# Two modulation vectors from plain float32 products, four channel chunks in the column groups of the array

## The chip, the core and the metric

The kernel is one program on one core of a Trainium2 chip. The metric is the device time of one execution in microseconds (us), here as the median of three runs. In the text PE is TensorE, DVE is VectorE, ACT is ScalarE, POOL is GpSimd and SP the engine that issues most loads. Numbers of the form L570 are lines of the kernel before; where the changed kernel is meant, the text says so.

## The reference, cut to what matters

The model is two transformer-like blocks on 256 tokens of width 2048 (and 256 context tokens). The change concerns its first step, the modulation: two conditioning vectors, `c` and `c_ctx`, go through SiLU and are multiplied with `w_mod`. Of the six vectors of 2048 that come out, the first two (shift and scale of the first norm) are needed for both conditioning vectors, before anything else can be projected:

```python
sil = silu([c, c_ctx])                        # 2 x 2048
mod = sil @ w_mod[:, 0:4096] + b_mod[0:4096]  # shift, scale: 2 x 2048 each
h   = rmsnorm(x,   norm1_w) * (1 + scale[0]) + shift[0]    # 256 x 2048
hc  = rmsnorm(ctx, norm1_w) * (1 + scale[1]) + shift[1]
p   = h @ w_in + b_in                         # q, k, v, gates of the mixer; same for hc
```

The result has to agree with float32 products. The kernel gets them in two ways: by splitting each operand into a high part in the type float32r and a rest, and adding three products of the parts; or by handing float32 operands to the array as they are.

## The kernel before, in words

Phase A, the first 198 us, is all that the change edits. `w_mod`'s first 4096 columns are stored as eight blocks of 512 columns, `wmodA[0..7]`; block b and block 4 + b are shift and scale of the same 512 channels. `mod_block(b)` goes through the 2048 input channels in 16 steps k of 128. Its weights come by `wstream`, a generator that loads four k at a time (`raw`, 128 x 4 x 512, one MB, L162, on the SP queue) and splits each k: ACT casts it to `whi` (L117) and DVE subtracts to get `wlo` (L118); both have four buffers. The stationary operand is `silx`, 128 x 4: high and low part of the two conditioning vectors. PE multiplies it with `whi` (L570) and with `wlo` (L571), 512 columns each, so that four rows of a PSUM bank hold the sums. ACT copies these to `mrow` (L573), and `mod_cols` turns them into columns by four small transposes (L579) and adds the parts and the bias on DVE (L581, L583).

The loop over the four channel chunks c calls `mod_block(c)`, `mod_block(4 + c)` and then queues `early(c)`, which does two things. `h_chunk(c)` makes the modulated `hTh` (ACT, L603), the same in float32 in place (POOL, L604) and the rest `hTl` (DVE, L605), eight instructions of each. Then four k of the first half of the key projection and four of the query projection follow (`ws_ka`, `ws_qa`): 24 and 12 products of 256 columns for each k, L189, 144 products a chunk. Before the first chunk `x_norm` loads x and ctx, scales them, and turns them by transposes (L207).

What stands where on each engine is set by a scheduler that takes the program's pieces in the order in which they are queued, and by buffers: 16 pages of 8 KB a partition (`page`), 2 `raw` buffers (`stm`), 19 small ones (`t2`), and 4 + 4 PSUM banks (`mmb`, `smb`). An engine does its instructions in the order of its own queue. `half_step` and `rate` say how many queued pieces are emitted with each k.

Of the kernel before, what the change touches and what calls it, by code (L numbers as in the profile page):

```python
# [33 lines left out]
def body(ctx, tc, A, out):  # L34
# [69 lines left out]
    def sq_part(ss, x, tt, j):  # L104
        """sum of squares of column block j of x[tt]"""
        junk = t2([128, 512], F32, "junk")
        nc.scalar.activation(out=junk[:], in_=x[tt][:, j * 512:j * 512 + 512], func=AF.Square, accum_out=ss[:, tt, j:j + 1])
# [12 lines left out]
    def due(then, X, at):  # L120
        """X, with then() emitted when its k first reaches at"""
        todo = [then]

        def X_(k, i):
            if todo and k >= at:
                todo.pop()()
            return X(k, i)

        return X_

    def warm(func):
        """the table of func, ahead of its use"""
        t = wk.tile([128, 1], F32, name="warm", tag="warm")
        tc.keep_in_program_order(nc.scalar.activation(out=t[:], in_=ones[:], func=func))
# [4 lines left out]
    def pump(n=1):  # L139
        """emit the next n pieces of the work that runs beside the weight streams"""  # L140
        for lane in lanes:
            m = n
            while m > 0 and lane:
                try:
                    with tc.issue_after(last_split[0].ins) if paced[0] else ExitStack():
                        next(lane[0])
                    m -= 1
                except StopIteration:
                    lane.pop(0)
# [59 lines left out]
    def token_row(r, name):  # L209
        """r [128, 2], tokens on partitions, as a row of 256 on every partition"""  # L210
        ps = smb()
        for tt in range(2):
            nc.tensor.matmul(ps[:, tt * 128:tt * 128 + 128], lhsT=r[:, tt:tt + 1].to_broadcast([128, 128]), rhs=ident[:],
                             start=True, stop=True)
        t = t2([128, 256], F32, name)
        nc.vector.tensor_copy(out=t[:], in_=ps[:, 0:256])
        return t

    def turned(xs, j):
        """column block j of xs, channel-major: two banks of two chunks"""  # L220
        for k2 in range(j * 4, j * 4 + 4, 2):
            ps = smb()
            for k in range(2):
                for tt in range(2):
                    transpose(ps[:, k * 256 + tt * 128:k * 256 + tt * 128 + 128],
                              xs[tt][:, (k2 + k) * 128:(k2 + k) * 128 + 128])
            yield k2, ps
# [14 lines left out]
    def chan_part(xs, j, gcol, chan):  # L242
        """column block j of xs with a factor per channel, channel-major and split"""
        for k2, ps in turned(xs, j):
            for k in range(2):
                kk = k2 + k
                (h_, l_), p_ = chan(kk, 0), ps[:, k * 256:k * 256 + 256]
                nc.scalar.activation(out=h_, in_=p_, func=AF.Copy, scale=gcol[:, kk:kk + 1])
                nc.vector.scalar_tensor_tensor(out=l_, in0=p_, scalar=gcol[:, kk:kk + 1], in1=h_.bitcast(F32),
                                               op0=OP.mult, op1=OP.subtract)  # L250

# [47 lines left out]
    def s5_prep():  # L299
# [23 lines left out]
        def horner(o, x, coefs, last):  # L323
            """o = (...((c0 x + c1) x + c2)...) x + last"""
            ts(o, x, coefs[0], None, OP.mult)
            for c_ in coefs[1:]:
                V.scalar_tensor_tensor(out=o, in0=o, scalar=c_, in1=x, op0=OP.add, op1=OP.mult)
            ts(o, o, last, None, OP.add)
# [51 lines left out]
        # unit rotation and decay of four steps, and the rotations at the starts of the chunks  # L380
# [34 lines left out]
        # powers of the transition  # L415
# [9 lines left out]
        # input coefficients  # L425
# [20 lines left out]
    def s5_prep2():  # L446
# [12 lines left out]
        # parity of the step: rows of a block-diagonal factor for two groups, and the products by lag after zeros  # L459
# [46 lines left out]
        for e in range(16):  # L506
# [15 lines left out]
            # with the conjugate of c its table is the one of Re(c z) up to the sign of the imaginary part  # L522
# [32 lines left out]
    silx = cst.tile([128, 16, 4], F32R, name="silx")  # L555
    split(silx[:, :, 0:2], silx[:, :, 2:4], sil[:])
# [9 lines left out]
    def mod_block(b):  # L566
        """512 modulation columns for both vectors, channel-major; high and low parts as rows of one product"""
        ps = smb()
        for k, wh, wl in wstream(A["wmodA"][b], 16, rawp=page if b else raw_first):
            nc.tensor.matmul(ps[0:4, :], lhsT=silx[:, k, :], rhs=wh, start=(k == 0), stop=False)  # L570
            nc.tensor.matmul(ps[0:4, :], lhsT=silx[:, k, :], rhs=wl, start=False, stop=(k == 15))  # L571
        mrow = t2([4, 512], F32, "mrow")
        nc.scalar.copy(out=mrow[:], in_=ps[0:4, :])  # L573
        bg.append(mod_cols(b, mrow))

    def mod_cols(b, mrow):
        pt = smb()
        for j in range(4):
            nc.tensor.transpose(pt[:, j * 4:j * 4 + 4], mrow[:, j * 128:(j + 1) * 128], ident[0:4, 0:4])  # L579
        p4 = pt[:, 0:16].rearrange("p (a b) -> p a b", b=4)  # L580
        nc.vector.tensor_tensor(out=modc[:, b], in0=p4[:, :, 0:2],  # L581
                                in1=bmod[:, b * 4:b * 4 + 4, None].to_broadcast([128, 4, 2]), op=OP.add)
        nc.vector.tensor_tensor(out=modc[:, b], in0=modc[:, b], in1=p4[:, :, 2:4], op=OP.add)  # L583
# [4 lines left out]
    def h_chunk(c):  # L588
        """channels 512 c .. 512 c + 511 of the modulated x and ctx"""
# [27 lines left out]
    # the first projections follow the modulation, chunk by chunk  # L617
# [41 lines left out]
    def mod_vector(v):  # L659
        """c-modulation vector v (2..5), as a row in memory; the scale of the second norm with its weight"""  # L660
# [34 lines left out]
    def mod_narrow(v, accs, step, eng):  # L695
        """the same in column blocks, up to the sums over partitions"""
# [93 lines left out]
    # differential attention  # L790
# [69 lines left out]
    def normed_turn(o, ss, factor, hi, lo, slow):  # L860
        """o scaled by its head norm and factor(tt, h), channel-major and split"""
# [14 lines left out]
    def to_chan(src, nk, hi, lo):  # L876
        """src(k, tt) token-major [128, 128] chunks -> hi/lo channel-major pages [128, nk, 256]"""
# [68 lines left out]
    # gate rows: direction * 32 + head on partitions, all 512 tokens  # L946
# [214 lines left out]
    def mod_col(v, name):  # L1161
        """modulation vector v by channel: [128, 16]"""
# [99 lines left out]
    # dense activations gelu(h2 . u), [i2, i1, t], two first keys i1 per unit, by way of memory  # L1262
# [20 lines left out]
    # slot[:, 0/1/2, t]: first key, second key and weight of each of a token's 128 slots, slots on partitions  # L1283
# [57 lines left out]
    def scatter(half, G):  # L1341
        """G[i2, i1, t] for 64 first keys: per token the product of the slots' one-hot rows, the weights in exact parts"""
# [33 lines left out]
    class Half:  # L1376
        """the products with expert_v of 64 first keys"""
# [38 lines left out]
        def run(self, done, after):  # L1416
            """the last two rows column block by column block, so that the ends of the blocks are spread"""
# [35 lines left out]
    def first_half():  # L1453
        """the first half's part of x2, once its gate is there"""
# [37 lines left out]
    # the norm that ends the first block and the one that begins the second, from two sums of squares  # L1492
# [35 lines left out]
    # 1 / rms of the first norm, and of both in one  # L1528
# [58 lines left out]
    # forget gates of the forgetting attention  # L1587
# [9 lines left out]
    # decay of the gated linear attention, channel-major  # L1597
# [33 lines left out]
    # gated linear attention: pairs (s, t) split by the level of the halving at which s and t part  # L1631
# [56 lines left out]
    # forgetting attention  # L1688
# [30 lines left out]
    # head norm of the gated linear attention, gates  # L1719
# [35 lines left out]
    def s5_v(h):  # L1755
        """the table of the inputs' part of the states of 16 groups, and what else s5_in needs"""
# [85 lines left out]
    def s5_u(h):  # L1842
        """u by (group of the pair, token in chunk from the last, channel of the group)"""
# [10 lines left out]
    def s5_in(h):  # L1854
        """states at the ends of the chunks of 4 tokens, of 16 groups"""
# [40 lines left out]
    def s5_out(h, U, X):  # L1896
        """outputs within and across chunks"""
# [25 lines left out]
    def s5_y(h):  # L1923
        """back to channels, skip and gelu"""
# [98 lines left out]
def _layout(inp):  # L2023
# [82 lines left out]
    # channels of 8 groups of 16 in the order (channel of the group, group)  # L2106
# [7 lines left out]
    # groups as (16 channel blocks in pairs, 8): a pair is the same group of the two blocks  # L2114
# [11 lines left out]
    # shape-only constants  # L2126
# [49 lines left out]
```

## Time and profile before

| what | value |
|---|---|
| median of three runs | 3814.56 us (3808.14 to 3821.2) |
| profiled execution | span 3811.4 us from its first to its last instruction; no other time is given for it |
| PE | busy 95% of the span, 24610 products |
| DVE | busy 72% |
| ACT | busy 49% |
| POOL | busy 21% |
| DMA | 754.22 MB, mean 198 GB/s |
| phase A, to the last product of the first query projection | 198.14 us |

A share over the whole span says little on phase A: there PE is busy 157.8 of 198.14 us, and the waits are in a few places. A product's row gives a duration that includes the filling and draining of the array; how often products follow each other is read from their starts. A plain float32 product leaves two records in the trace, one for each of two passes.

### The profile page before, as it was taken

The page shows a single profiled execution, that of the slowest core. Times are in us where ns is not written, and L with a number is a line of the kernel's source. Part 1 is how long each engine was busy: PE and PEld are TensorE (multiplying, and loading weights), DVE is VectorE, ACT ScalarE, POOL GpSimd, SP SyncE. Part 2 cuts the span into 40 slices and gives each one's busy share as a digit, 9 for nine tenths or more (in the row PEclk, how much of TensorE's full clock was granted, in tenths as well). Part 3 has the DMA queues.
Part 4 walks back from the last instruction along what each step waited for, and adds up shares of the span by engine and source line. Part 5 has one row for each costly group of instructions (what it writes and reads, how often), then busy time and mean ns, then how long its engine had stood idle before and what let it go on. Part 6 is the DMA issues. An engine that isn't in the chain of part 4 may idle for free.

```text
span 3811.4 us, 65434 instructions
## 1 busy us (share of the span) xinstructions
PE 3638.0 (95%) x24610; PEld 3172.0 (83%) x24610; DVE 2744.6 (72%) x4697; ACT 1859.4 (49%) x3748; POOL 792.1 (21%) x778
## 2 busy tenths in 40 slices
PE   7899999999999999999999998899999999988998
PEld 4698878887789999999877888888879977787896
DVE  6765897777658687887787589866577676676765
ACT  7622544654455444555545445554454445433464
POOL 1211210100101022554011057300032021242300
PEclk8999999999999999999999999999999999999999
DMA  8464564367654555555667534666545635776554
GB/s 329 175 241 171 179 234 151 110 247 292 236 198 146 196 197 188 199 189 190 240 232 257 189 136 161 241 219 212 193 162 190 204 116 177 214 202 188 156 194 166
DMA packets 155246, 754.22 MB, mean 198 GB/s; under 512 B 40609, under 2 KB 40897, under 8 KB 76465
## 3 DMA queue, kind: packets, MB, share of 16 engines
q1 hardware_dynamic: 116224, 661.78, 49.4%
q0 software_dynamic: 29232, 84.07, 6.9%
q10 hardware_dynamic: 9472, 4.20, 0.4%
q8 instruction: 192, 3.15, 0.3%
q14 instruction: 126, 1.02, 0.1%
HBM read 716.65 MB, written 33.19 MB: 197 GB/s over the span
## 4 chain that ended last, share of the span: by engine, by line
PE 77%; DVE 9%; DMA 5%; issue 3%; POOL 3%; ACT 3%; DVEq 0%; ACTq 0%; POOLq 0%; SPq 0%
PE mm L189 15%; PE mm L180 7%; PE mm L183 7%; PE mm L181 7%; PE sm L1273 5%; PE sm L1274 5%; PE sm L1278 5%; PE mm L1414 3%; PE sm L1411 3%; PE mm L1411 3%; PE sm L1414 3%; PE sm L1412 3%; PE mm L1412 3%; DVE wlo L118 3%; POOL oh L1354 1%
## 5 line engine op out<-in xcount | busy, mean ns | idle before, releaser
L118 DVE TENSOR_TENSOR wlo<-raw,whi 128x512 fp32r<-128x512 f32 x2224 | 1647.7, 760 | 833.8 <-ACT whi L117 745.6
L117 ACT CAST whi<-raw 128x512 fp32r<-128x512 f32 x2224 | 1349.2, 620 | 1613.6 <-PE mm L181 333.3
L1273 PE MATMUL sm<-h2h,whi 128*128 128x256 f32 x2048 | 514.2, 283 | 0.5 <-ACT whi L117 0.5
L1274 PE MATMUL sm<-h2l,whi 128*128 128x256 f32 x2048 | 509.0, 282 | 0.0
L1273 PEld LDWEIGHTS sm<-h2h,whi 128*128 128x128 f32 x2048 | 388.0, 189 | 0.7 <-ACT whi L117 0.7
L1274 PEld LDWEIGHTS sm<-h2l,whi 128*128 128x128 f32 x2048 | 387.7, 189 | 0.0
L1278 PE MATMUL sm<-h2h,wlo 128*128 128x256 f32 x2048 | 327.5, 282 | 10.3 <-DVE wlo L118 10.3
L1354 POOL TENSOR_TENSOR oh<-e,gpart 128x512 bf16<-128x512 bf16 x192 | 281.7, 1491 | 136.9 <-ACT whi L117 62.4
L1278 PEld LDWEIGHTS sm<-h2h,wlo 128*128 128x128 f32 x2048 | 279.8, 189 | 11.7 <-DVE wlo L118 11.5
L180 PE MATMUL mm<-whi,hTh 128*128 128x512 f32 x576 | 229.6, 399 | 0.7 <-ACT whi L117 0.4
L181 PE MATMUL mm<-whi,hTl 128*128 128x512 f32 x576 | 227.0, 394 | 0.0
L189 PE MATMUL mm<-hTh,whi 128*128 128x256 f32 x704 | 178.9, 289 | 6.0 <-ACT whi L117 3.5
L189 PE MATMUL mm<-hTl,whi 128*128 128x256 f32 x704 | 175.7, 284 | 0.0
L183 PE MATMUL mm<-wlo,hTh 128*128 128x512 f32 x576 | 172.6, 397 | 1.5 <-DVE wlo L118 1.4
L189 PEld LDWEIGHTS mm<-hTh,whi 128*128 128x128 f32 x704 | 134.4, 191 | 15.7 <-ACT whi L117 5.3
L189 PE MATMUL mm<-cnh,whi 128*128 128x256 f32 x512 | 137.4, 300 | 3.6 <-ACT whi L117 3.6
L189 PEld LDWEIGHTS mm<-hTl,whi 128*128 128x128 f32 x704 | 134.7, 192 | 3.2 <-issue 1.5
L180 PEld LDWEIGHTS mm<-whi,hTh 128*128 128x128 f32 x576 | 108.5, 188 | 30.2 <-issue 3.4
L183 PEld LDWEIGHTS mm<-wlo,hTh 128*128 128x128 f32 x576 | 108.1, 189 | 28.3 <-DVE wlo L118 3.6
L189 PE MATMUL mm<-cnl,whi 128*128 128x256 f32 x512 | 131.0, 288 | 0.0
L181 PEld LDWEIGHTS mm<-whi,hTl 128*128 128x128 f32 x576 | 108.5, 188 | 23.3
L1281 POOL DMA_DIRECT2D scr_a<-ua x64 | 36.3, 567 | 432.7 <-ACT ua L1280 421.3
(1564 smaller groups left out, 7949.8 us busy)
## 6 DMA issues: line engine op xcount, KB each, us to landing
raw<-in_u_t_dram SPq DMA_DIRECT2D x128, 1024.0 KB, 4.8
raw<-in_expert_v_dram SPq DMA_DIRECT2D x124, 1024.0 KB, 4.8
raw<-in_w_in_dram SPq DMA_DIRECT2D x80, 1024.0 KB, 4.9
raw<-in_ab_w_in_dram SPq DMA_DIRECT2D x56, 1024.0 KB, 4.9
raw<-in_wmodA_dram SPq DMA_DIRECT2D x32, 1024.0 KB, 7.2
mraw<-in_wmodB_dram SPq DMA_DIRECT2D x32, 1024.0 KB, 8.4
raw<-in_c_w_in_dram SPq DMA_DIRECT2D x32, 1024.0 KB, 5.1
mrn<-in_wmodB_dram POOLq DMA_DIRECT2D x64, 256.0 KB, 3.9
```

Source lines behind the costliest of these rows:

```text
L117: nc.scalar.copy(out=hi, in_=src)
L118: last_split[0] = nc.vector.tensor_tensor(out=lo, in0=src, in1=hi.bitcast(F32), op=OP.subtract)
L180: nc.tensor.matmul(o, lhsT=xh, rhs=wh, start=(k == 0), stop=False)
L181: nc.tensor.matmul(o, lhsT=xl, rhs=wh, start=False, stop=False)
L183: nc.tensor.matmul(ps[i][:], lhsT=X(k, tt)[0], rhs=wl, start=False, stop=(k == K - 1))
L189: nc.tensor.matmul(o, lhsT=w[:, j * 128:(j + 1) * 128], rhs=x, start=start, stop=stop, skip_group_check=True)
L1273: nc.tensor.matmul(o, lhsT=uh, rhs=xh, start=(k == 0 and r == 0), stop=False, skip_group_check=True)
L1274: nc.tensor.matmul(o, lhsT=uh, rhs=xl, start=False, stop=False, skip_group_check=True)
L1278: nc.tensor.matmul(o, lhsT=w_, rhs=x_, start=False, stop=(k_ == 15 and r == 1), skip_group_check=True)
L1354: nc.gpsimd.tensor_tensor(out=oh1[i][:], in0=e1[:], in1=gpart[:, i, tb:tb + 8, None].to_broadcast([128, 8, 64]), op=OP.mult)
L1411: nc.tensor.matmul(self.ps[tt][b][:], lhsT=hl[tt][0], rhs=vh, start=first, stop=False)
L1412: nc.tensor.matmul(self.ps[tt][b][:], lhsT=hl[tt][1], rhs=vh, start=False, stop=False)
```

## The change

`silx` with its split goes. A zeroed operand `silz` of 32 columns for each k, of which two hold the conditioning vectors, takes its place. `mod_block` loads the same `raw` pieces in the same order on the same queue, but multiplies them unsplit, in float32: the four k of a piece go to four groups of 32 columns of the array, and their sums to four groups of 32 partitions of one bank. `mod_cols` then transposes four full 128 x 128 blocks, and adds up the four groups in a DVE reduction. The rest of the diff takes comments and docstrings away. After phase A, the order of the instructions on each engine is the same in both kernels.

```diff
-    silx = cst.tile([128, 16, 4], F32R, name="silx")
-    split(silx[:, :, 0:2], silx[:, :, 2:4], sil[:])
+    silz = t2([128, 16, 32], F32, "silz")
+    nc.gpsimd.memset(silz[:], 0.0)
+    nc.vector.tensor_copy(out=silz[:, :, 0:2], in_=sil[:])
...
     def mod_block(b):
         ps = smb()
-        for k, wh, wl in wstream(A["wmodA"][b], 16, rawp=page if b else raw_first):
-            nc.tensor.matmul(ps[0:4, :], lhsT=silx[:, k, :], rhs=wh, start=(k == 0), stop=False)
-            nc.tensor.matmul(ps[0:4, :], lhsT=silx[:, k, :], rhs=wl, start=False, stop=(k == 15))
-        mrow = t2([4, 512], F32, "mrow")
-        nc.scalar.copy(out=mrow[:], in_=ps[0:4, :])
+        for k4 in range(0, 16, 4):
+            raw = (page if b else raw_first)("raw", [128, 4, 512])
+            nc.sync.dma_start(out=raw[:], in_=A["wmodA"][b][:, k4:k4 + 4, :])
+            for k in range(4):
+                half_step[0] += rate[0] / 2
+                pump(int(half_step[0]))
+                half_step[0] -= int(half_step[0])
+            for k in range(4):
+                nc.tensor.matmul(ps[32 * k:32 * k + 32, :], lhsT=silz[:, k4 + k, :], rhs=raw[:, k, :], start=(k4 == 0),
+                                 stop=(k4 == 12), tile_position=(0, 32 * k), skip_group_check=True)
+        mrow = t2([128, 512], F32, "mrow")
+        nc.scalar.copy(out=mrow[:], in_=ps[:])
         bg.append(mod_cols(b, mrow))
 
     def mod_cols(b, mrow):
         pt = smb()
         for j in range(4):
-            nc.tensor.transpose(pt[:, j * 4:j * 4 + 4], mrow[:, j * 128:(j + 1) * 128], ident[0:4, 0:4])
-        p4 = pt[:, 0:16].rearrange("p (a b) -> p a b", b=4)
-        nc.vector.tensor_tensor(out=modc[:, b], in0=p4[:, :, 0:2],
-                                in1=bmod[:, b * 4:b * 4 + 4, None].to_broadcast([128, 4, 2]), op=OP.add)
-        nc.vector.tensor_tensor(out=modc[:, b], in0=modc[:, b], in1=p4[:, :, 2:4], op=OP.add)
+            transpose(pt[:, j * 128:(j + 1) * 128], mrow[:, j * 128:(j + 1) * 128])
+        nc.vector.tensor_reduce(out=modc[:, b], in_=pt[:].rearrange("p (j g v) -> p j v g", j=4, g=4)[:, :, 0:2, :],
+                                axis=AX.X, op=OP.add)
+        nc.vector.tensor_tensor(out=modc[:, b], in0=modc[:, b], in1=bmod[:, b * 4:b * 4 + 4, None].to_broadcast([128, 4, 2]),
+                                op=OP.add)
         yield
```

PE in the first chunk's key projection, before: between projection products (`hTh`, `hTl` with `whi`, `wlo`; the numbers name buffers) stand pairs of modulation products, one pair for each k.

```order
L189 MATMUL mm<-hTh_544,wlo 128x256
L189 MATMUL mm<-hTh_542,wlo 128x256
L189 MATMUL mm<-hTh_544,wlo 128x256
L570 MATMUL sm<-whi,silx 4x512
L571 MATMUL sm<-wlo,silx 4x512
L570 MATMUL sm<-whi,silx 4x512
L571 MATMUL sm<-wlo,silx 4x512
L189 MATMUL mm<-hTh_542,whi 128x256
```

PE in the same projection, changed kernel (its L578 are the modulation products, straight from `raw`).

```order
L189 MATMUL mm<-hTh_376,wlo 128x256
L189 MATMUL mm<-hTh_378,wlo 128x256
L189 MATMUL mm<-hTh_376,wlo 128x256
L189 MATMUL mm<-hTh_378,wlo 128x256
L578 MATMUL sm<-raw,silz 32x512 x4
L189 MATMUL sm<-hTh_376,whi 128x256
```

The pairs are gone; a whole piece of four k stands as one run of four products.

DVE at the start of the first chunk, before: after the scale `amod` the rests `hTl` of the modulated input, and between them splits `wlo` of weights.

```order
L591 SCALAR_TENSOR_TENSOR amod<-modc,nw_79 128x8
L118 TENSOR_TENSOR wlo<-raw,whi 128x512 x2
L605 TENSOR_TENSOR hTl_543<-xnT_87,hTh_542 128x256
L605 TENSOR_TENSOR hTl_545<-xnT_89,hTh_544 128x256
L605 TENSOR_TENSOR hTl_543<-xnT_87,hTh_542 128x256
L605 TENSOR_TENSOR hTl_545<-xnT_89,hTh_544 128x256
L118 TENSOR_TENSOR wlo<-raw,whi 128x512 x4
L605 TENSOR_TENSOR hTl_543<-xnT_87,hTh_542 128x256
L605 TENSOR_TENSOR hTl_545<-xnT_89,hTh_544 128x256
L118 TENSOR_TENSOR wlo<-raw,whi 128x512 x2
L605 TENSOR_TENSOR hTl_543<-xnT_87,hTh_542 128x256
```

DVE at the same place in the changed kernel, from `amod` of the first chunk to the first reduction of the second (its L599, L613 and L588).

```order
L599 SCALAR_TENSOR_TENSOR amod<-modc,nw_79 128x8
L613 TENSOR_TENSOR hTl_377<-xnT_87,hTh_376 128x256 x2
L613 TENSOR_TENSOR hTl_379<-xnT_89,hTh_378 128x256 x2
L613 TENSOR_TENSOR hTl_377<-xnT_87,hTh_376 128x256
L613 TENSOR_TENSOR hTl_379<-xnT_89,hTh_378 128x256
L613 TENSOR_TENSOR hTl_377<-xnT_87,hTh_376 128x256
L613 TENSOR_TENSOR hTl_379<-xnT_89,hTh_378 128x256
L118 TENSOR_TENSOR wlo<-raw,whi 128x512 x8
L588 TENSOR_REDUCE modc<-sm 128x8
```

Only the eight splits of the projections' own weights are left, and they stand behind all `hTl` of the chunk.

## Rows read from the trace of the kernel before

**Rows 1.** The page: the span, and each engine's busy time over it.
```profile
span 3811.4 us, 65434 instructions
PE 3638.0 (95%) x24610; PEld 3172.0 (83%) x24610; DVE 2744.6 (72%) x4697; ACT 1859.4 (49%) x3748; POOL 792.1 (21%) x778
```

**Rows 2.** Busy time by stretch, cut at each chunk's first `hTh`; last: clock, DMA, GB/s.
```profile
0.00:56.66 56.66, 34.64 (x138) 15.55 (x138) 30.75 (x73) 41.34 (x92) 8.97 (x20) 0.82 0.97 385
56.66:100.68 44.02, 37.35 (x221) 25.70 (x222) 32.35 (x57) 30.20 (x56) 8.05 (x10) 0.88 0.72 261
100.68:137.66 36.98, 33.64 (x216) 23.37 (x215) 29.17 (x53) 26.81 (x49) 10.45 (x10) 1.00 0.65 238
137.66:178.49 40.83, 33.18 (x212) 23.38 (x210) 29.68 (x53) 28.01 (x50) 8.87 (x13) 0.92 0.33 117
178.49:198.14 19.65, 18.99 (x145) 18.72 (x146) 8.22 (x15) 10.68 (x21) 6.91 (x9) 0.91 0.31 109
```

**Rows 3.** Groups of phase A (0 to 198.14): busy us, mean ns, idle before, releasers.
```profile
L118 DVE TENSOR_TENSOR wlo<-raw,whi 128x512 fp32r<-128x512 f32 x163 | 105.5, 689 | 33.0 <-ACT whi L117 26.1 <-PE sm L571 6.4
L117 ACT CAST whi<-raw 128x512 fp32r<-128x512 f32 x164 | 94.8, 619 | 46.3 <-PE sm L570 16.0 <-PE mm L189 10.7 <-PE sm L189 8.5
L570 PE MATMUL sm<-whi,silx 128*4 128x512 f32 x128 | 56.7, 443 | 21.2 <-ACT whi L117 20.1 <-ACT mrow L573 0.9
L571 PE MATMUL sm<-wlo,silx 128*4 128x512 f32 x128 | 56.2, 439 | 9.0 <-DVE wlo L118 8.7
```

**Rows 4.** Chain of waits, first chunk: start us, us, what.
```profile
58.37 3.45 POOL xnT L604 x4
...
62.32 2.44 POOL xnT L604 x3
...
65.13 0.69 DVE wlo L118
...
65.87 0.59 PE sm L571
```

**Rows 5.** Chain of waits, fourth chunk.
```profile
176.79 0.60 PE sm L579 x8
...
178.49 0.61 ACT hTh L603
...
179.15 13.34 PE mm L189 x96
192.48 5.65 PE sm L189 x48
```

**Rows 6.** Timeline of PE, one pair in a dense stretch: start us, us, line.
```profile
82.21 0.40 PE L570 MATMUL sm<-whi,silx 128*4 128x512 f32 x1
82.44 0.40 PE L571 MATMUL sm<-wlo,silx 128*4 128x512 f32 x1
82.69 0.27 PE L189 MATMUL mm<-hTh,whi 128*128 128x256 f32 x1
```

**Rows 7.** Timeline of PE: two float32 products in two halves of the rows.
```profile
501.39 1.13 PE L811 MATMUL sm<-ka,qa 64*128 64x512 f32 x4
502.45 0.38 PE L189 MATMUL mm<-hTl,whi 128*128 128x256 f32 x1
```

**Rows 8.** The same, cut to 501.395 to 501.9.
```profile
501.39 0.70 PE L811 MATMUL sm<-ka,qa 64*128 64x512 f32 x2
```

**Rows 9.** Timeline of PE: four float32 products, all rows, one column.
```profile
324.90 3.59 PE L685 MATMUL sm<-macc,ones 128*1 128x512 f32 x8
328.42 0.50 PE L180 MATMUL mm<-whi,hTh 128*128 128x512 f32 x1
```

**Rows 10.** Timeline of PE: eight float32 products of 32 columns, then full ones.
```profile
2849.37 1.08 PE L542 MATMUL sm<-s5c,s5bd 128*32 128x64 f32 x16
2850.38 0.51 PE L180 MATMUL mm<-whi,abh 128*128 128x512 f32 x1
2850.72 0.40 PE L181 MATMUL mm<-whi,abl 128*128 128x512 f32 x1
2850.96 0.39 PE L180 MATMUL mm<-whi,abh 128*128 128x512 f32 x1
```

**Rows 11.** L117's instructions alone, 45.94 to 56.66: ACT busy, clock, DMA, GB/s.
```profile
45.94:56.66 10.72, 5.61 (x10) 0.68 1.01 413
```

**Rows 12.** Timeline of PE: full transposes, at full clock.
```profile
42.32 0.93 PE L207 MATMUL sm<-ident,xt 128*128 128x128 f32 x7
```

## The prediction

> **What bounds the kernel now.** I read the page first: PE is busy 95% of 3811.4 us [rows 1], so work taken from PE, or a wait on PE, counts nearly one for one, and work taken from DVE (72%) or ACT (49%) counts only where PE waits for it. The order of instructions differs in phase A alone, so I then cut that phase at the first `hTh` of each chunk [rows 2]. The reader is to see five stretches. In the first, to 56.66, the DMA engines are full (share 0.97, 385 GB/s): loading bounds it, with PE busy 34.64 us. The next three, one for each chunk, take 44.02, 36.98 and 40.83 us, together 121.8, with PE busy 33 to 37 us in each and the DMA share falling to 0.33: there PE and its waits bound. The last, 19.65 us, holds the fourth chunk's projections and no modulation.
>
> The chain of waits shows what PE waits for in the middle stretches. POOL makes its part of `h`, 3.45 and 2.44 us; DVE's `hTl` wait for POOL; behind them in DVE's queue stands a `wlo` of a modulation block, and only at 65.87 does PE get its L571 [rows 4]. In the last stretch nothing of the kind stands between: `hTh` at 178.49, products from 179.15 to 198.14 [rows 5].
>
> **The change, part by part.** *Splits.* 128 of 164 casts on ACT and as many of the 163 subtractions on DVE go [rows 3]: 128 x 0.619 = 79 us and 128 x 0.689 = 88 us of engine time. None of it is a term by itself; its worth is that PE's modulation products then wait for a load only. 21.2 and 9.0 us of idle PE stand before L570 and L571 [rows 3], some of which will turn into waits for `hTl` instead.
>
> *Products.* Before, a pair L570, L571 takes 82.69 - 82.21 = 0.48 us [rows 6], four pairs for a `raw` piece 1.92. After, a piece is four float32 products, eight records of 512 columns. One record alone takes (328.42 - 324.90) / 8 = 0.44 us [rows 9]; at 32 output columns it is no faster, since 16 records of 64 columns need 1.01 us to the next product [rows 10], 0.063 a record, or 0.50 for eight times the columns with the switch in it. So eight records one after the other cost 3.5 us. What they cost side by side in column groups no row shows; the ends are two passes with all four abreast, 0.88, and 3.5. The nearest row is L811: two float32 products, each in one half of the array's rows, put four records into 502.45 - 501.39 = 1.06 us [rows 7], where one after the other would be 1.76. And in the first half microsecond two records are there, both over by 0.70 us [rows 8]: the first passes of both products ran together, then both second passes. I take that for four groups too: 1.06 for a piece. Added to it is the switch back to the full array: after L542 the first full product takes 2850.72 - 2850.38 = 0.34 to the next, against 0.24 after it [rows 10], so 0.1. Together 1.17 us a piece, against 1.92.
>
> Here the Trainium skill has a rule that speaks against the value: TensorE: Matmul & The Clock Gate, Part 3: Packing small matmuls, says that matmuls start and end in program order. If a product's two passes stand together in that order, the second pass of one product would have to start before the first pass of the next; by that rule L811's starts would be staggered, and they are not [rows 8], so the trace differs. The same section reports 2.38 times the speed for three column groups, which would make four abreast an estimate of about 1.1 us; no run here shows column groups yet.
>
> *Transposes and sums.* Eight small transposes a chunk took 0.60 us [rows 5]; eight full ones take 8 x 0.93 / 7 = 1.06 [rows 12]. The DVE sums stay two short instructions. The copy `mrow` has 128 partitions in place of 4 with the same 512 columns, so I count it as equal. The zeroing of `silz` on POOL lies beside the first load.
>
> *A chunk after the change.* The fourth chunk of before, 19.65 us from its first `hTh` to its last projection product [rows 2], is a chunk without splits in the way, with POOL's eight instructions and a slow-clock start (0.91) included. To it I add eight pieces, 8 x 1.17 = 9.4, the transposes, 1.0, and the way from the last modulation product over copy, sums and scale to `hTh`: 178.49 - 176.79 = 1.7 from the transposes on [rows 5], plus a copy of 0.6, less the transposes that I have counted, rounded up to 2.2 for hand-overs. That is 32.3 us a chunk, 96.9 for three: 24.9 less than 121.8. Loading does not stop it: a chunk needs ten pieces of 1.049 MB (eight of modulation, two of projections), 25.4 us at 413 GB/s [rows 11].
>
> *The first stretch.* In the 10.7 us before the first `hTh`, ACT spends 5.61 on ten casts [rows 11] that stand in its queue among the copies which `hTh` needs. They go; I take the whole 5.6, so `hTh` starts near 51. Loading allows it: eight modulation pieces, four of x and ctx and three of projections are 15.7 MB, 41 us at 385 GB/s.
>
> *The sum.* 24.9 + 5.6 = 30.5 us. What follows phase A keeps its order, and PE is what limits it, so I carry all of it to the end: 3811.4 - 30.5 = 3780.9 for an execution like the profiled one. The median of the runs stands 3.2 above that span: **3784**. Ends of this case: if the waits at chunk starts stay as they are (40.6 a chunk on the mean less 144 x 0.118 = 17.0 of projections at the rate of the 48 products in [rows 5], less 15.4 of pairs, less 0.6, leaves 7.6), a chunk takes 35.1 and the gain is 22; if four streams need 1.6 a piece, it is 20, with both 12. If nearly all waits go, a chunk comes to 28.8 and the gain to 41. So 3773 to 3803.
>
> **Rivals.** *In order, two abreast.* Only the second pass of one product and the first of the next overlap: five slots of 0.44, with the switches of L811 (1.06 - 0.88 = 0.18) and 0.1, 2.5 us a piece. A chunk is then 42.9, three lose 6.9, the first stretch still gives 5.6: 3816, no change. Against it speaks [rows 8]. The rule of the Trainium skill's page TensorE: Matmul & The Clock Gate, Part 3, would give this case.
>
> *One after the other.* The column groups share one stream of the moving operand, so nothing overlaps: 3.6 us a piece with the switch, 51.7 a chunk, 155 for three, 33 lost; with pieces arriving every 2.5 us the first stretch gains nothing either. 3848, slower. It decides from about 2.4 us a piece upward: there the 24 pieces of three chunks, at 2.4 - 1.17 more each, have eaten the 30.5. For it: no row shows four streams through the same rows. Against it: L811 gains as much from two groups as passes allow.
>
> *The saving is lost.* Pages are freed by PE now, not by DVE, so a late piece can hold the next load; or the stretch after phase A begins to wait for loads that had been early. Against it: ten pieces need 25.4 of 32.3 us, and that stretch's loads go out when it begins. It would leave about 5 us of gain: 3810.
>
> **How the numbers follow.** Four abreast 0.62, in order 0.15, one after the other 0.13, lost 0.10. What runs of this kernel can tell from no change is about 0.3%, 11.4 us. Four abreast falls to the faster side but for a few hundredths; of the rest, lost lies half there. Faster 0.66; same 0.17, mostly the in-order case and half of lost; slower 0.17, the serial case and the bad end of the in-order one. The range from 3768 to 3818 takes in the first case whole, most of the in-order case, and the lost one; the serial case, 0.13, stays outside.
>
> **What would show it.** In the changed trace, L578's records: four starting within some tens of ns, 0.5 us apart from the next four, is the first case; pairs are the second; single starts 0.43 us apart the third. The first `hTh` of the chunks should stand near 51, 83, 116 and 148 us, and the last projection product near 168. The chain at chunk starts should run over `hTl` to L189, with no `wlo` before a modulation product. DMA should stay near its full rate to about 65 us. I am wrong if a piece takes over 2 us on PE, if the chunks stay at 40 us with PE idle, or if the gain at 168 us is not there at the end.

## The result and the profile after

The changed kernel takes **3764.2 us** (median of 4 runs, 3760.4 to 3766.2) against 3814.2 for the kernel before on the same chip: a ratio of 0.9867, 95% interval 0.9854 to 0.9881. The forecast was 3784, range 3768 to 3818. The direction is right and the gain is 50.0 us instead of 30.5, so the time lies below the range.

| | before | forecast | after |
|---|---|---|---|
| time, us (median) | 3814.2 | 3784 | 3764.2 |
| span of the profiled execution, us | 3811.4 | 3780.9 | 3764.5 |
| a `raw` piece on PE, us | 1.92 | 1.17 | 0.99 |
| first `hTh` of the chunks, us | 56.7, 100.7, 137.7, 178.5 | 51, 83, 116, 148 | 58.6, 88.8, 118.8, 149.4 |
| last projection product of phase A, us | 198.1 | 168 | 169.7 |

First the page, as in [rows 1]: span and busy time of the engines.

```profile
span 3764.5 us, 64975 instructions
PE 3589.0 (95%) x24610; PEld 3151.5 (84%) x24610; DVE 2660.7 (71%) x4569; ACT 1786.7 (47%) x3619; POOL 786.9 (21%) x779
```

Then phase A cut at each chunk's first `hTh`, the columns as in [rows 2].

```profile
0.00:58.64 58.64, 28.80 (x144) 14.69 (x144) 12.97 (x44) 25.84 (x61) 10.85 (x22) 0.83 0.97 385
58.64:88.82 30.18, 28.09 (x220) 19.76 (x216) 9.71 (x21) 10.19 (x19) 7.31 (x10) 1.00 0.88 339
88.82:118.78 29.96, 28.13 (x220) 19.71 (x216) 9.71 (x21) 10.18 (x18) 7.30 (x10) 1.00 0.79 289
118.78:149.36 30.58, 27.35 (x212) 19.51 (x208) 9.80 (x21) 10.18 (x19) 8.38 (x12) 1.00 0.55 207
149.36:169.69 20.33, 19.49 (x145) 19.03 (x146) 8.22 (x15) 10.69 (x21) 6.92 (x9) 0.92 0.16 58
```

A chunk with modulation now takes 30.2, 30.0 and 30.6 us, of which PE is busy all but 2 to 3; before, 3 to 8 us of each were idle [rows 2]. The first stretch has not become shorter, although ACT and DVE do much less in it. Phase A as a whole ends 198.14 - 169.69 = 28.45 us earlier.

The chain of waits at the second chunk's start answers to [rows 4]: `hTh`, POOL, `hTl`, product, and no `wlo` of a modulation block in between.

```profile
58.64 0.61 ACT hTh L611
...
61.53 0.44 DVE hTl L613
61.97 0.04 issue
62.01 4.63 PE mm L189 x37
66.65 0.99 PE sm L578 x8
67.64 2.48 PE mm L189 x19
```

PE's timeline at the piece in it, as in [rows 8]: first cut after half a microsecond, then the whole piece.

```profile
66.58 0.64 PE L578 MATMUL sm<-raw,silz 128*32 128x512 f32 x4
...
66.58 1.07 PE L578 MATMUL sm<-raw,silz 128*32 128x512 f32 x8
67.57 0.39 PE L189 MATMUL mm<-hTh,wlo 128*128 128x256 f32 x1
```

Four records are over by 67.22, four more follow, and the next product starts at 67.57. In a single column group records follow each other 0.44 us apart (the run with one group, below), so four that overlap are one of each product, and its second record comes behind them. The four column groups do run side by side.

That accounts for 28 of the 47 us between the spans. Most of the others appear where the order of instructions is the same in both kernels: in the products with `expert_v`, 3072 float32r products of 512 columns in two halves (`mms` of `Half`). Here are 100 us from the middle of the second half, of the kernel before and then of the changed one (the columns of the windows: length, then PE, PEld, DVE, ACT, POOL busy with their instructions, clock, DMA share, GB/s).

```profile
2600.00:2700.00 100.00, 100.00 (x430) 80.17 (x429) 60.54 (x90) 49.32 (x81) 0.00 (x0) 1.00 0.62 212
```

```profile
2600.00:2700.00 100.00, 100.00 (x443) 82.81 (x442) 58.71 (x87) 49.37 (x81) 0.00 (x0) 1.00 0.60 210
```

PE is never idle and its clock is 1.00 in both; yet there are 430 products in one and 443 in the other. A window also counts the record that reaches into it, and a record is some 0.39 us long, so the products stand 100.39 / 430 = 233.5 and 100.39 / 443 = 226.6 ns apart, where one product more or less in the count is 0.5 ns. Their starts in the window, read one by one, give 233.3 and 226.7: 6.7 ns, or 20.5 us over 3072 products. The whole stage agrees: from the first start to the last, the first half takes 360.97 us before (1840.66 to 2201.63) and 352.77 after (1814.66 to 2167.43), the second 370.72 (2430.50 to 2801.22) and 359.77 (2396.12 to 2755.89), together 19.1 us less. The page's busy share can't show this, since PE is at 95% in both.

### The profile page after: what moved, and what is told of

The parts are those of the page before. It is cut to its first block, busy times and chain, and to the rows that moved or that the text cites. A ratio compares the mean times of both kernels' runs of the same rounds, so it can differ in the third digit from the quotient of the medians.

```text
span 3764.5 us, 64975 instructions
## 1 busy us (share of the span) xinstructions
PE 3589.0 (95%) x24610; PEld 3151.5 (84%) x24610; DVE 2660.7 (71%) x4569; ACT 1786.7 (47%) x3619; POOL 786.9 (21%) x779
## 4 chain that ended last, share of the span: by engine, by line
PE 77%; DVE 9%; DMA 5%; issue 4%; POOL 3%; ACT 2%; DVEq 0%; ACTq 0%; POOLq 0%; SPq 0%
PE mm L189 15%; PE mm L180 7%; PE mm L183 7%; PE mm L181 7%; PE sm L1281 5%; PE sm L1282 5%; PE sm L1286 5%; PE mm L1422 3%; PE sm L1422 3%; PE mm L1419 3%; PE sm L1420 3%; PE mm L1420 3%; PE sm L1419 3%; DVE wlo L118 3%; POOL oh L1362 1%
## 5 line engine op out<-in xcount | busy, mean ns | idle before, releaser
L118 DVE TENSOR_TENSOR wlo<-raw,whi 128x512 fp32r<-128x512 f32 x2096 | 1567.3, 765 | 844.1 <-ACT whi L117 749.9
L117 ACT CAST whi<-raw 128x512 fp32r<-128x512 f32 x2096 | 1274.5, 621 | 1607.9 <-PE mm L181 319.8
```

The costliest lines, as they stand in the source:

```text
L117: nc.scalar.copy(out=hi, in_=src)
L118: last_split[0] = nc.vector.tensor_tensor(out=lo, in0=src, in1=hi.bitcast(F32), op=OP.subtract)
```

## Experiments

**What was open.** Removing `silx`, and taking `silz` as the first of the work tiles (tag t2), moves every tile in SBUF. In the compiled programs the moving tiles `whi` and `wlo` begin at multiples of 128 bytes in both kernels. The work tiles, among them the stationary `wh_` and `wl_` of the expert products, begin 64 bytes past such a multiple before (187968), because two small tiles of 32 bytes stand ahead of them, and at one after (187648). Theory A: this place sets the 233 or 227 ns. Theory B: the place of moving tiles or pages. Theory C: the rotation of the work tiles, or the moment at which the stage begins.

### Work tiles 64 bytes higher in the changed kernel

```diff
+    gap = wk.tile([128, 16], F32, name="gap", tag="gap", bufs=1)
+    nc.gpsimd.memset(gap[:], 0.0)
     cT = cload("cT", [128, 16, 2], eng=nc.sync)
```

> The changed kernel with a tile of 64 bytes a partition put ahead of the work tiles, so that these alone (the stationary wh_ and wl_ of the expert products among them) begin 64 bytes higher, at 64 past a multiple of 128 as in the kernel before; every other tile stays where it is. Theory A (the expert products go faster in the changed kernel because its stationary tiles begin at multiples of 128 bytes): they stand 233 ns apart again instead of 227, and the time rises by 3072 x 6.4 ns = 19.6 us, to 3784 us. Theory B (the moving tiles' place, or that of the pages, decides): 227 ns and 3764 us. Theory C (the order in which the work tiles rotate through their slots, or the moment at which the stage begins): 227 ns and 3764 us.

Measured: 3788.1 us, ratio to before 0.9926 (0.9914 to 0.9938), 23.9 us slower than the changed kernel (the kernel before stood at 3814.3 beside this run and at 3814.2 beside that one). The same 100 us:

```profile
2600.00:2700.00 100.00, 100.00 (x430) 80.58 (x429) 57.96 (x86) 48.53 (x79) 0.00 (x0) 1.00 0.59 203
```

430 again, and the two halves take 730.1 us in place of 712.5. B and C are out as far as this kernel goes.

### All tiles 256 bytes higher in the changed kernel

```diff
+    gap = cst.tile([128, 64], F32, name="gap")
+    nc.gpsimd.memset(gap[:], 0.0)
     cT = cload("cT", [128, 16, 2], eng=nc.sync)
```

> The changed kernel with a tile of 256 bytes a partition among the constants, so that the moving tiles, the pages and the work tiles all begin 256 bytes higher: the moving tiles and the pages lie where they lie in the kernel before, the work tiles still at multiples of 128 bytes. Theory A (alignment of the stationary work tiles): 227 ns between expert products and 3764 us. Theory B (place of moving tiles and pages): 233 ns and 3784 us. Theory C (rotation or moment): 227 ns and 3764 us.

Measured: 3761.6 us, ratio 0.9867 (0.9853 to 0.9881), and 443 products in that window, as in the changed kernel:

```profile
2600.00:2700.00 100.00, 100.00 (x443) 82.84 (x442) 56.94 (x84) 48.61 (x79) 0.00 (x0) 1.00 0.59 208
```

Moving tiles and pages lie where they lie in the kernel before, and the gain is still there: B is out.

### Work tiles 64 bytes lower in the kernel before

```diff
+            junk = t2([128, 512], F32, "junk")
             ss4 = wk.tile([128, 1, 4], F32, name="ss4", tag="ss4")
             for j in range(4):
-                junk = t2([128, 512], F32, "junk")
+                junk = t2([128, 512], F32, "junk") if j else junk
```

> The kernel before, its modulation unchanged, with the work tiles alone 64 bytes lower, at multiples of 128 (a small tile is allocated behind the first of them instead of ahead). Theory A: 227 ns between expert products instead of 233, and 3814 - 19.6 = 3794.6 us with nothing of the change in it. Theories B and C: 233 ns and 3814 us.

Measured: 3791.8 us, ratio 0.9945 (0.9933 to 0.9957): 22.5 us faster with nothing of the change in it. The window:

```profile
2600.00:2700.00 100.00, 100.00 (x443) 82.79 (x442) 60.56 (x91) 50.13 (x82) 0.00 (x0) 1.00 0.63 216
```

The two halves take 713.1 us in place of 731.7: 18.6 of the 22.5 us, whose interval runs from 16 to 26. The 20 us are thus no consequence of the column groups or of the missing split; two lines that only change the order of two allocations bring them to the old kernel as well.

### The products alone, by the place of their operands

Behind the last store, 128 products a line, with nothing on the other engines; `cols(off, n, w)` takes `w` columns of one aligned float32r page from column `off + n * w` (16 columns are 64 bytes).

```diff
+    for n in range(128):
+        nc.tensor.matmul(bp[n % 4][:], lhsT=cols(16, n % 16, 128), rhs=cols(0, n // 8 % 4, 512), start=True, stop=True)
```

> The changed kernel with 640 float32r products of 512 columns put behind its last store, with nothing beside them on the other engines: 128 with stationary and moving operand both at multiples of 128 bytes, 128 with the stationary 64 bytes past one, 128 with the moving one 64 past, 128 with both, 128 with the stationary 32 past. Theory A (the stationary operand's start decides): 227 ns apart in the first and third group, 232 to 234 in the second and fourth, the fifth not known beforehand. Rival D (what decided in the runs that shifted the work tiles were the writes of VectorE and ScalarE into them): 227 ns in all five. Rival B (the moving operand): the third and fourth are the slow ones.

Measured, 25 us of each group in this order (stationary and moving operand past a multiple of 128 bytes by 0 and 0, 64 and 0, 0 and 64, 64 and 64, 32 and 0), of the first group behind its start at a lower clock:

```profile
3758.00:3783.00 25.00, 25.00 (x112) 20.71 (x111) 0.00 (x0) 0.00 (x0) 0.00 (x0) 1.00 0.00 0
3786.00:3811.00 25.00, 25.00 (x108) 20.15 (x108) 0.00 (x0) 0.00 (x0) 0.00 (x0) 1.00 0.00 0
3815.00:3840.00 25.00, 25.00 (x111) 20.53 (x110) 0.00 (x0) 0.00 (x0) 0.00 (x0) 1.00 0.00 0
3845.00:3870.00 25.00, 25.00 (x112) 20.72 (x111) 0.00 (x0) 0.00 (x0) 0.00 (x0) 1.00 0.00 0
3874.00:3899.00 25.00, 25.00 (x108) 20.14 (x108) 0.00 (x0) 0.00 (x0) 0.00 (x0) 1.00 0.00 0
```

Nothing else runs here, and two groups are still slow (108), so it is not VectorE's or ScalarE's writes (rival D). But theory A fails in the fourth group: both operands at 64 give 25.39 / 112 = 226.7 ns, the fast value, as both at 0 do. The next two runs ask whether the place of one operand relative to the other decides (A2).

### Both operands moved by 64 bytes, in the kernel and alone

In the changed kernel with the 256 bytes of the second experiment made 64 (`[128, 16]`):

> The changed kernel with 64 bytes a partition among the constants, so that moving tiles, pages and work tiles all begin 64 bytes higher: the expert products' stationary tiles and moving tiles both at 64 past a multiple of 128. The measurement behind the last store had both at 64 at 227 ns, which the absolute place of the stationary alone does not explain. Theory A (the stationary's own place decides): 233 ns and 3784 us, as with the work tiles alone shifted. Theory A2 (it is the place of the stationary relative to the moving operand, modulo 128): 227 ns and 3764 us.

Measured: 3764.0 us, ratio 0.9877 (0.986 to 0.9893), 443 products in the window:

```profile
2600.00:2700.00 100.00, 100.00 (x443) 82.80 (x442) 57.55 (x85) 48.72 (x79) 0.00 (x0) 1.00 0.59 205
```

And alone, in seven groups:

> The changed kernel with 896 float32r products of 512 columns behind its last store, in seven groups of 128, stationary and moving operand past a multiple of 128 bytes by: 64 and 64, 0 and 64, 64 and 0, 32 and 32, 0 and 0, 32 and 64, 0 and 32. Theory A2 (relative place): 227 ns in the first, fourth and fifth group, 229 to 234 in the others. Theory A (the stationary's own place): 227 in the second, fifth and seventh, 233 in the others. If the order in the stretch and not the place decided in the first such measurement: no pattern by these offsets.

```profile
3759.00:3784.00 25.00, 25.00 (x112) 20.68 (x111) 0.00 (x0) 0.00 (x0) 0.00 (x0) 1.00 0.00 0
3786.00:3811.00 25.00, 25.00 (x111) 20.50 (x110) 0.00 (x0) 0.00 (x0) 0.00 (x0) 1.00 0.00 0
3815.00:3840.00 25.00, 25.00 (x109) 20.15 (x108) 0.00 (x0) 0.00 (x0) 0.00 (x0) 1.00 0.00 0
3845.00:3870.00 25.00, 25.00 (x112) 20.70 (x111) 0.00 (x0) 0.00 (x0) 0.00 (x0) 1.00 0.00 0
3874.00:3899.00 25.00, 25.00 (x112) 20.69 (x111) 0.00 (x0) 0.00 (x0) 0.00 (x0) 1.00 0.00 0
3903.00:3928.00 25.00, 25.00 (x109) 20.08 (x108) 0.00 (x0) 0.00 (x0) 0.00 (x0) 1.00 0.00 0
3933.00:3958.00 25.00, 25.00 (x109) 20.09 (x108) 0.00 (x0) 0.00 (x0) 0.00 (x0) 1.00 0.00 0
```

These are 64 and 64 (again behind a start at a lower clock), 0 and 64, 64 and 0, 32 and 32, 0 and 0, 32 and 64, 0 and 32. One product more or less in such a count is 2.1 ns, so the spacing is better read from the starts of the last 101 products of each group. Equal places give 226.7 ns in all five groups of the two runs; 64 and 0 (in both), 32 and 0, 32 and 64, and 0 and 32 give 233.3; 0 and 64 gives 228.9 in both. Theory A2 holds in all twelve groups as to which are slower, and A in its first form is dropped. A2 does not give the size: 64 and 0 lie as far apart modulo 128 as 0 and 64, and cost three times as much. The expert products of the kernel before were of the slow kind, 64 and 0.

### One column group in place of four

```diff
-                nc.tensor.matmul(ps[32 * k:32 * k + 32, :], lhsT=silz[:, k4 + k, :], rhs=raw[:, k, :], start=(k4 == 0),
-                                 stop=(k4 == 12), tile_position=(0, 32 * k), skip_group_check=True)
+                nc.tensor.matmul(ps[0:32, :], lhsT=silz[:, k4 + k, :], rhs=raw[:, k, :], start=(k4 + k == 0),
+                                 stop=(k4 + k == 15), tile_position=(0, 0), skip_group_check=True)
```

The copy, the transposes and the sum then take 32 rows.

> The changed kernel with all 16 k of a block in one column group (32 columns, one sum) instead of four side by side; the plain float32 products and the missing split stay. If the column groups are what makes a piece short, a piece of four k takes 4 x 0.9 = 3.6 us instead of 0.99, and the 24 pieces behind the first chunk alone cost 24 x 2.6 = 62 us, the 8 of the first chunk up to 21 more: 3826 to 3847 us, slower than the kernel before. If leaving the split out is what shortens the stage, and the products hide behind the loads and the first projections: under 3790 us.

Measured: 3807.8 us, ratio 0.9985 (0.9976 to 0.9994). PE's timeline of a piece and the first two chunks:

```profile
65.95 3.62 PE L578 MATMUL sm<-raw,silz 128*32 128x512 f32 x8
69.50 0.50 PE L189 MATMUL mm<-hTh,wlo 128*128 128x256 f32 x2
```

```profile
58.72:107.07 48.35, 47.68 (x217) 24.44 (x216) 9.60 (x21) 10.17 (x19) 7.33 (x10) 1.00 0.65 234
107.07:155.29 48.22, 47.55 (x217) 24.39 (x216) 9.65 (x21) 10.16 (x19) 7.30 (x10) 1.00 0.49 175
```

A piece takes 69.50 - 65.95 = 3.55 us, as expected, and phase A ends at 221.31. The first chunk's eight pieces cost nothing (its `hTh` stands at 58.72, within 0.1 of the changed kernel). The total is even 18 us under the expected range, whose lower end held 62 us for the other 24 pieces. Phase A grew by 221.31 - 169.69 = 51.6 us: PE, now busy through the whole chunk, also swallows most of the 2 to 3 us that it had waited, so a chunk grows by 17 to 18 us, not by 8 x 2.56 = 20.5. Behind phase A the profiled execution made up 4.5 us more (spans of 3811.6 and 3764.5), and it was itself 5.6 us slower than this kernel's median; no run looked for these. Against the kernel before, phase A is 23 us longer; the whole is not slower because the faster expert products are in it too. In phase A, plain float32 without the column groups is a loss.

### The splits kept, their results unread

```diff
+                hi = stm.tile([128, 512], F32R, name="whi", tag="whi", bufs=NSP)
+                lo = stm.tile([128, 512], F32R, name="wlo", tag="wlo", bufs=NSP)
+                split(hi[:], lo[:], raw[:, k, :])
```

> The changed kernel with every modulation block still split on ScalarE and VectorE as before, the two parts then read by nobody: the products stay plain float32, four abreast. If the shorter products on TensorE are what shortens the chunks: chunks stay near 30 us and the time at 3764 to 3768. If the missing splits shorten them (hTh and hTl no longer queue behind the casts and wlo of a piece): chunks of 35 to 41 us as before and 3779 to 3795 us.

Measured: 3774.5 us, ratio 0.9899 (0.9884 to 0.9914): between the two. The three chunks:

```profile
56.45:98.03 41.58, 33.78 (x236) 22.59 (x231) 34.47 (x63) 33.53 (x62) 8.58 (x10) 0.88 0.75 287
98.03:128.37 30.34, 27.21 (x204) 19.57 (x204) 25.08 (x48) 22.97 (x43) 7.93 (x10) 1.00 0.68 251
128.37:167.55 39.18, 29.18 (x212) 21.80 (x204) 28.76 (x53) 27.78 (x50) 8.87 (x13) 0.87 0.41 150
```

PE's timeline at the first of them shows what it waits for (in brackets the idle time before, and what ended it):

```profile
63.13 0.58 PE L189 MATMUL mm<-hTh,whi 128*128 128x256 f32 x1 [5.51 <-ACT whi L117]
...
66.79 1.22 PE L189 MATMUL mm<-hTh,wlo 128*128 128x256 f32 x4 [1.58 <-DVE wlo L118]
```

The casts and subtractions of the projection's own weights stand in the queues behind those of the modulation, and PE, idle, then starts at a lower clock (0.88). Phase A ends at 186.26: the splits cost 16.6 of the 28.5 us though nobody reads them, and the chunk between is as short as without them. At the end of the profiled executions 8.6 us of the 16.6 are left (3773.1 against 3764.5); no run looked for where the others went. Neither reading of the expectation is right alone: the missing split is worth the larger part, but only with products that are short enough to let it show (the run before this one).

### The norms issued earlier

`norm(i + 1)` (sums, factor, scaling) is issued after the second of the four groups of transposes of tile `i` instead of behind the fourth:

```diff
+                if k4 == 1 and i < 3:
+                    norm(i + 1)
```

> The changed kernel with the sums, the factor and the scaling of each tile of x and ctx issued between the two halves of the transposes of the tile before it, not behind them; loads at their old places. Theory N (in the changed kernel the first stretch is a chain of four norms, one behind the other in the queues of ScalarE and TensorE, 11.8 us a tile from one junk to the next, and the modulation's casts were not on it): the last tile is scaled near 43 us instead of 52, the first hTh stands at 48 to 50 us, bound by the last modulation piece that lands at 45.8, and the time falls by 8 to 10 us, to 3754 to 3756. Rival L (the loads set the first stretch): first hTh stays near 58 and the time at 3764.

Measured: 3756.8 us, ratio 0.9851 (0.9838 to 0.9865), first `hTh` at 53.57. Expected were 48 to 50: theory N is right in kind and was worth half of what it promised. Rival L is out for these 5 us, since the loads stood at their old places. ScalarE's `junk` of the last tile, then VectorE's scaling, then PE's transposes:

```profile
41.48 1.07 PE L584 MATMUL sm<-raw,silz 128*32 128x512 f32 x8 [0.48 <-DMA raw<-in_wmodA_dram]
41.56 0.64 ACT L266 ACTIVATE junk<-xt 128x512 f32<-128x512 f32 x1
...
45.73 1.29 DVE L271 TENSOR_SCALAR xt<-xt,rs_r 128x2048 f32<-128x2048 f32 x1
...
47.17 1.94 PE L207 MATMUL sm<-ident,xt 128*128 128x128 f32 x8 [4.62 <-DVE xt L271]
```

The last tile's chain still begins only at 41.56 and ends behind a wait of PE of 4.62 us.

To see whether the gain reaches the end, the changed kernel and this one were run again side by side.

> The changed kernel as it is, for a comparison on one chip with the next: 3764 us and a first hTh at 58.6 us by every theory.

> The kernel with the norms issued between the transposes, a second time, beside the changed kernel on the same chip. If the 5.1 us that its first hTh came sooner are carried to the end: 5 to 8 us under the changed kernel of the same call, 3756 to 3759. If they are lost on the way: 3764, within 2 us of it.

Measured: 3760.8 (0.9864, 0.9847 to 0.988) and 3757.5 us (0.9858, 0.9842 to 0.9875), with the first `hTh` at 59.07 and 55.19. 3.3 us, less than expected and within what these runs can tell from nothing. It is the fastest kernel here, but that it beats the changed one is not shown.

## Why the prediction was wrong, point by point

- **"I carry all of it to the end"** is the step that failed. The forecast looked at the order of instructions behind phase A, found it unchanged, and took their durations as unchanged too. The edit moved the work tiles by 64 bytes modulo 128 against the moving tiles, and 3072 products came to stand 6.7 ns closer. The two halves took 19.1 us less; moving the work tiles alone was worth 23.9 us of the median in one kernel and 22.5 in the other. Phase A alone came out near its forecast, 28.45 us against 30.5.
- **Products, 1.17 us a piece**: measured 0.99. The mechanism was right: first passes of all four together, then all second passes. The 1.06 was taken from L811, and the switch of 0.1 was added to it; the two passes and the switch together are within 0.99. (1.06 and 0.1 are 1.16, not 1.17.) The Trainium skill (TensorE: Matmul & The Clock Gate, Part 3: Packing small matmuls) gives 2.38 times for three column groups. Here four give 3.55 / 0.99 = 3.6 times. The four first passes shown above, ahead of all second passes, again rule out the prediction's reading of that section's rule of program order, in which a product's two passes stand together. The rule itself, taken product by product, can hold beside these records.
- **A chunk, 32.3 us**: measured 30.2 on the mean of three, 31 less than 121.8 in place of 24.9. Eight pieces at 0.18 less are 1.4 us of the 2.1; the rest, 0.6, no run takes apart. What a chunk owes to the missing split and what to the short products can't be added up: with the one alone it takes 48, with the other alone 30 to 42.
- **The first stretch, 51 us**: wrong; 58.64, 2 us later than before. The ten casts on ACT [rows 11] did go, but of the chain before they were only 0.53 us:

```profile
47.51 0.59 PE sm L571
...
54.44 0.24 PE sm L571
54.70 0.58 ACT mrow L573
55.28 0.95 ACT xnT L284 x2
56.23 0.53 ACT whi L117
```

  From 47.51 to 54.68 this chain is PE's modulation products and transposes, from 47.50 to 52.50 at a granted clock of 0.50. In the changed kernel the chain runs through the norms of the four tiles of x and ctx, one behind the other, and through pieces at a lower clock:

```profile
34.56 2.56 ACT junk L271 x8
...
38.73 1.30 DVE xt L276
40.03 0.14 issue
40.17 1.94 PE sm L207 x8
42.11 1.86 PE sm L578 x8
43.97 1.91 PE sm L207 x8
...
46.39 2.56 ACT junk L271 x8
```

  From one `junk` to the next are 11.83 us, and a piece takes 1.86 instead of 0.99, since PE, idle for 5.31 us ahead of 40.17, works at the lower of its two levels, 1.2 GHz, afterwards (granted clock 0.50 from 40.00 to 46.00). Busy time of ACT ahead of `hTh` was taken for waiting time.
- **Phase A**: forecast 30.5, measured 28.45. The errors in it, 7.6 too much at the start, 6.2 too little in the chunks, and a last stretch longer by 0.7 (20.33 against 19.65), nearly cancel. That this term came out so close is luck.
- **What is left open**: followed at the same product in both traces, the changed kernel is ahead by 28.4 us at the end of phase A, 26.0 at the first expert product, 34.2 at the end of the first half, 45.3 at the end of the second, and 46.9 at the end. So 2.4 us are lost between phase A and the expert products, and 1.6 won behind them. No run looked for these; the changed kernel's second profiled execution has a span of 3759.5, 5.0 us less than the first, so amounts of this size can't be given a cause.

The rivals: two abreast and one after the other did not occur, and the run with one group shows what the second would have cost. "The saving is lost" did not occur either. No rival held a gain larger than that of phase A: the list had only ways to lose.

## What to carry to other kernels

When an edit adds, drops or resizes a tile, or changes which tile is allocated first, compare the starts of stationary and moving operands modulo 128 before and after; the code order says nothing about it. Shown is this for float32r products that fill PE. In a stage that PE fills, count products in a window of the trace: the busy share stays at 100 whether there are 430 or 443. Engine time ahead of an event is worth something only if the chain of waits to that event runs through it, and two terms that enable each other are to be priced together.

## What the runs showed of the hardware that was not expected

- Float32r products of 128x128 by 512 columns at full clock stand 226.7 ns apart when stationary and moving operand begin at the same place modulo 128 bytes (0 and 0, 32 and 32, 64 and 64), 233.3 when they begin 64 or 32 bytes apart (64 and 0, 32 and 0, 32 and 64, 0 and 32, stationary first), and 228.9 for 0 and 64. The Trainium skill (SBUF — State Buffer, A bandwidth-pool intuition that's wrong) gives weight loads a second, independent read port. In these runs what the place of one operand costs depends on the place of the other, which two wholly independent reads would not show; by what path they meet is not shown.
- Eight records of float32 products of 512 columns in four column groups of 32 take 0.99 us, in one group 3.55 us. One such record takes 0.44 us, about twice the 0.227 of a float32r product, so that a float32 product passes through the array only twice is not shown: the two "passes" of this text are its two records.
